# Layer 0's recurrence rates, computed in the projection stage for all tokens and read back from DRAM

## The chip, the cores and the metric

The kernel runs on one core of a Trainium2 chip. Five engines work side by side: PE (TensorE, matmuls), DVE (VectorE), ACT (ScalarE), POOL (GpSimd) and SP (SyncE, which issues the DMAs here). The metric is the device time of one execution in microseconds, median over runs; lower is better. TensorE's clock is granted by a throttle: 1.00 in a row means 2.4 GHz, 0.50 means 1.2 GHz.

## The reference

The program is a block with four mixers and a feed-forward part, then two layers with a mixer and a mixture of experts each. Layer 0's mixer has a recurrence ("rw", of the RWKV-7 kind) beside a latent attention (MLA). The change touches the rates of that recurrence. Cut to it:

```python
def rwkv_prep(p, prm):
    p = centred_shift_mix(p, prm['mu'])
    r, k, v, w1f, w1b, a1f, a1b, g1 = jnp.split(p, RW_SPLITS, axis=-1)
    ...
    for d, (w1, a1) in enumerate(((w1f, a1f), (w1b, a1b))):
        z = (prm['w0'][d] + jnp.tanh(w1) @ prm['w2'][d]).astype(jnp.float32)
        decay = jnp.exp(-jnp.exp(-jax.nn.softplus(-z) - 0.5))
        a = jax.nn.sigmoid((prm['a0'][d] + a1 @ prm['a2'][d]).astype(jnp.float32))
        k_d = kf * (1.0 + (a - 1.0) * prm['k_a'])
        dirs.append((heads(decay), heads(k_d), -kk, kk * heads(a)))
    g = jax.nn.sigmoid(g1) @ prm['g2']
    return heads(r), heads(v), dirs, g
```

`decay` and `a` are the rates: for each of two directions d, a 64 x 512 matrix turns 64 numbers per token into 512. The kernel computes both sigmoids as tanh(0.5 z), 768 tokens (256 of context, 512 latent), 512 channels in four blocks m of 128.

## The kernel before, in words

Layer 0's mixer (`l0_mixer`) has two stages that matter here.

**The projection stage** (`l0_proj`, about 781 to 1066 us of the trace) multiplies the normed tokens with a wide input matrix, 128 output columns at a time. One `project` is 48 matmuls into one PSUM tile of role `p2` (two tiles of two banks each are all that this role has; `p1` has one-bank tiles). `mixed` then blends each token with its neighbours: ACT makes `mc` from PSUM (L989), DVE `ms` (L992) with a POOL copy of the edges (L994), and DVE the result (L995), which is the last reader of the PSUM tile. The first two projections give `tw` (the tanh'd inputs w1 of both directions, then a1): rows 0 to 63 belong to direction 0, rows 64 to 127 to direction 1. They are stored to DRAM as `twT`. The next one is the gate (`sgh`, `sgl`, then six matmul triples with `g2`, copied by ACT at L1020 and stored to `gtok`), then four for k (k0 to k3, with a small fp32 norm matmul on `ind`, L1056), and so on. In front of each projection `fill` lets one or two pieces of the two layers' ada modulation go (L882: four matmuls of 32 output rows and 512 columns per piece, from weights that arrive by DMA). Weights are split into a high and a low part (`wload`: ACT makes `abw_hi` at L208, DVE `abw_lo` at L209), so every product is three matmuls (L186 to L188).

**The recurrence stage** (`l0_rwkv`, about 1066 to 1540 us) walks over six pairs of chunks j, one pair holding 128 tokens of each direction. `rw_prep(j)` loads r, k1, k2 and kk of the chunk (`ld...`, four DMAs of 256 KB for each direction) and makes `ar` and `bk` from them and the rates, mostly on DVE: L1516, a scan at L1519, exponentials on ACT (L1525, L1527), then L1531 to L1538. The step after it is the gram matmul (L1571, which needs `ar` and `bk`). MLA attention steps (s, L186 to L188, softmax, L1269, L1276) are put between by the order string ORD1, which starts `A0 m2 B0 m1 C0 m1 D0 m1 A1`. The rates of chunk pair j are made by `rw_rates(j)`, called once ahead of the loop and then at the end of `rw_prep(j - 1)`: per pair four DMAs of `tw` (32 KB each) out of `twT`, 16 fp32 matmuls with 64 rows of contraction and 128 columns (L1475; each shows as two records) into PSUM tiles `g`, and 16 tanh of 128x128 (L1480) into the tiles `th0`, `th1`. The matrices `w2` and biases `w0` are loaded by `rw_setup` (L1420 to L1427).

The tile scheduler orders the instructions of each engine within a stage; buffers and data decide what waits.

Of the kernel before, what the change touches and what calls it, by code (L numbers as in the profile page):

```python
# [9 lines left out]
F32 = mybir.dt.float32  # L10
# [3 lines left out]
AF = mybir.ActivationFunctionType  # L14
OP = mybir.AluOpType
# [4 lines left out]
P = 128  # L20
# [65 lines left out]
class Net:  # L86
# [828 lines left out]
    def l0_mixer(self, x, xpool, opool, xd, xs):  # L915


        nc, tc = self.nc, self.tc
        d = self.dram
        T = 768  # L920
# [11 lines left out]
        self.twT = d.tile([2, P, T], F32, name="twT")  # L932
# [4 lines left out]
        with ExitStack() as es:  # L937
# [5 lines left out]
            for t in (0, 1, 3, 4, 2, 5):  # L943
# [3 lines left out]
                pv, ts = pt.rearrange("p (i t) -> p i t", i=4), slice(t * P, (t + 1) * P)  # L947
# [3 lines left out]
    def l0_proj(self, x, xpool):  # L951
        nc, I, tc = self.nc, self.I, self.tc
        T = 768
        w = I["ab_w_in_2"][0]
        with ExitStack() as es:
# [19 lines left out]

            def project(wh, wl, j, m=P):

                self.fill(5)
                o = self.p2()
                for k in range(8):  # L980
                    for (a, b) in ((256, 768), (0, 256)):
                        self.mm3(o[:m, 256 + a:256 + b], wh[:, k, j:j + m], wl[:, k, j:j + m],
                                 hi[:, k, a:b], lo[:, k, a:b], k == 0, k == 7)
                return o[:m, 256:1024]
# [13 lines left out]
            wh, wl = self.wload(w, 8, 256, "abw", c0=12 * P)  # L998
            for j in range(2):
                m = wp.tile([P, T], F32, tag="mx", bufs=3, name="mx")  # L1000
                mixed(project(wh, wl, j * P), 12 + j, m)
                if j == 0:
                    nc.scalar.activation(m, m, AF.Tanh)
                nc.sync.dma_start(self.twT[j], m)
# [339 lines left out]
    def l0_rwkv(self, xd, xs, es):  # L1344
        nc = self.nc

        with ExitStack() as e2:
            self.rc = e2.enter_context(self.pool("rwc", 1))
            self.rw = e2.enter_context(self.pool("rww", 2))
            with self.pool("rwp", 2) as self.rp, self.pool("mla", 1, "right") as mp:  # L1350
# [4 lines left out]
                self.rw_rates(0)  # L1355

# [61 lines left out]
    def rw_setup(self):  # L1418
        nc, I, rc = self.nc, self.I, self.rc
        self.w2 = rc.tile([P, 2, 512], F32, name="w2")  # L1420
        self.w0 = rc.tile([P, 2, 2, 4], F32, name="w0")
        for i, (w, o) in enumerate((("rw_w2_2", "rw_w0_2"), ("rw_a2_2", "rw_a0_2"))):
            nc.sync.dma_start(self.w2[:, i], I[w][0].rearrange("d k n -> (d k) n"))
            src = I[o][0]
            nc.sync.dma_start(self.w0[:, i], bass.AP(tensor=src.tensor, offset=src.offset,
                                                     ap=[[1, P], [512, 2], [P, 4]]))
        nc.vector.tensor_scalar(self.w0, self.w0, 0.5, None, op0=OP.mult)  # L1427
# [32 lines left out]
    def rw_rates(self, j):  # L1460

        nc, rp = self.nc, self.rp
        if j == 6:
            return
        self.rth = []
        for d in range(2):
            seg = self.chunks(2 * j)[d] // 2
            ts, hs = slice(seg * P, (seg + 1) * P), slice(64 * d, 64 * d + 64)
            th = []
            for i in range(2):  # L1470
                tw = rp.tile([P, P], F32, tag=f"tw{i}", bufs=1, name=f"tw{i}")
                nc.sync.dma_start(tw[hs], self.twT[i, hs, ts])
                z = self.pt("g")
                for m in range(4):
                    nc.tensor.matmul(z[:, m * P:(m + 1) * P], self.w2[hs, i, m * P:(m + 1) * P], tw[hs],  # L1475
                                     start=True, stop=True)
                t = rp.tile([P, 512], F32, tag=f"th{i}{d}", bufs=1, name=f"th{i}")
                for m in range(4):
                    cs = slice(m * P, (m + 1) * P)
                    nc.scalar.activation(t[:, cs], z[:, cs], AF.Tanh, scale=0.5, bias=self.w0[:, i, d, m:m + 1])  # L1480
                th.append(t)
            self.rth.append(th)
# [19 lines left out]
    def rw_prep(self, j):  # L1502
# [4 lines left out]
        for d in range(2):  # L1507
# [7 lines left out]
            th, ta = self.rth[d]  # L1515
# [26 lines left out]
        self.rw_rates(j + 1)  # L1542
# [876 lines left out]
```

## Time and profile before

| what | value |
|---|---|
| median of 3 runs | 2537.07 us (2532.33 to 2540.72) |
| the profiled execution | 2529.52 us, span 2527.8 us |
| mean granted clock | 0.929 |
| PE busy | 2277.4 us, 90% of the span |
| DVE, ACT, POOL busy | 1545.7, 1109.3, 321.7 us |

The span is the stretch that the trace covers; the execution's own time is 1.7 us longer. All working is done against the profiled execution, which lies 7.6 us under the median of the runs.

### The profile page before, as it was taken

To read this page: it belongs to the slowest core of one execution; us is meant where nothing else is said; L and a number is where in the kernel's file an instruction comes from. 1 tells how busy PE (TensorE), PEld (TensorE's weight loads), DVE (VectorE), ACT (ScalarE), POOL (GpSimd) and SP (SyncE) were. 2 spreads that over 40 slices of the span, in tenths; PEclk is the share of its full clock that TensorE was granted. 3 is DMA by queue.
4 is the path that set the end of the run, shared out by engine and by line. 5 is a ranking of instruction groups with operands and counts; after the bars stand their busy time and mean duration, and the time that the engine had idled before them with its cause. 6 is when DMAs were issued, how large, how long until landed. Compare 5 with 4: busy or idle time off the path is not lost. (4 is left out here: it accounts for less than half of the span.)

```text
span 2527.8 us, 37507 instructions
## 1 busy us (share of the span) xinstructions
PE 2277.4 (90%) x14345; PEld 1808.3 (72%) x14345; DVE 1545.7 (61%) x2915; ACT 1109.3 (44%) x1836; POOL 321.7 (13%) x409
## 2 busy tenths in 40 slices
PE   8959999999988999988999998898994989998994
PEld 6836577888876677766788886697773767687773
DVE  4455654323324455645676648967876987666885
ACT  4435533212223233433445433336774456624773
POOL 0001201000000000011111114200113113301112
PEclk9979989999999999955999999989997999998997
DMA  5345535233325656453545426639996220056995
GB/s 166 100 166 173 190 136 196 88 109 100 101 61 189 224 191 218 125 125 73 113 112 124 102 59 183 236 130 341 342 340 225 97 67 1 1 171 206 375 365 191
DMA packets 367793, 411.55 MB, mean 163 GB/s; under 512 B 117476, under 2 KB 299172, under 8 KB 361468
## 3 DMA queue, kind: packets, MB, share of 16 engines
q1 hardware_dynamic: 356972, 370.83, 46.4%
q0 software_dynamic: 10640, 38.31, 4.1%
q8 instruction: 114, 1.87, 0.3%
q14 instruction: 67, 0.55, 0.1%
HBM read 340.46 MB, written 70.65 MB: 163 GB/s over the span
## 5 line engine op out<-in xcount | busy, mean ns | idle before, releaser
L304 DVE TENSOR_REDUCE mx<-s 128x1 f32<-128x768 f32 (+4 forms) x160 | 121.4, 760 | 85.9 <-PE s L188 65.3
L209 DVE TENSOR_TENSOR eg_l<-eg_w,eg_h 128x2048 fp32r<-128x2048 f32 x66 | 151.0, 2289 | 19.5 <-ACT eg_h L208 19.3
L208 ACT ACTIVATE eg_h<-eg_w 128x2048 fp32r<-128x2048 f32 x66 | 126.5, 1918 | 28.7 <-DMA eg_w<-in_moe_w_up_dram 12.2
L186 PE MATMUL p<-lhh,abw_hi 128*128 128x512 f32 (+1 forms) x336 | 115.3, 343 | 0.8 <-ACT l0n1tmp L241 0.8
L188 PE MATMUL p<-lhh,abw_lo 128*128 128x512 f32 (+1 forms) x336 | 114.5, 341 | 1.6 <-DVE abw_lo L209 1.6
L187 PE MATMUL p<-lhl,abw_hi 128*128 128x512 f32 (+1 forms) x336 | 114.7, 341 | 0.0
L187 PE MATMUL g<-eg_l,xh 128*128 128x512 f32 x264 | 107.1, 406 | 5.5 <-DVE eg_l L209 5.0
L186 PE MATMUL g<-eg_h,xh 128*128 128x512 f32 x264 | 107.6, 408 | 3.8 <-ACT eg_h L208 3.8
L188 PE MATMUL g<-eg_h,xl 128*128 128x512 f32 x264 | 104.4, 395 | 0.0
L209 DVE TENSOR_TENSOR ed_l<-ed_w,ed_h 128x2048 fp32r<-128x2048 f32 x33 | 75.6, 2292 | 44.1 <-ACT ed_h L208 44.1
L882 PE MATMUL adaps<-adaw,silu_c 128*32 128x512 f32 x384 | 75.3, 640 | 29.6 <-DMA adaw<-in_ada_w_dram 29.6
L994 POOL COPY ms<-mc 128x2 f32<-128x2 f32 x30 | 9.1, 304 | 635.0 <-ACT mc L989 620.1
L2025 POOL DMA_INDIRECT xe<-h2d,idx x33 | 45.9, 1392 | 310.0 <-PE x L2039 243.4
L186 PEld LDWEIGHTS p<-lhh,abw_hi 128*128 128x128 f32 (+1 forms) x336 | 61.8, 184 | 23.9 <-issue 8.0
L310 POOL TENSOR_SCALAR ap<-ap,rc 128x768 f32<-128x768 f32 x64 | 58.4, 913 | 153.7 <-DVE rc L307 92.0
L310 POOL TENSOR_SCALAR mlp<-mlp,rc 128x768 f32<-128x768 f32 (+1 forms) x48 | 41.5, 864 | 250.8 <-DVE rc L307 200.4
L186 PE MATMUL p<-h2h,wg_hi 128*128 128x512 f32 x176 | 69.5, 395 | 0.6 <-ACT h2h L234 0.6
L188 PEld LDWEIGHTS p<-lhh,abw_lo 128*128 128x128 f32 (+1 forms) x336 | 62.3, 185 | 10.1 <-DVE abw_lo L209 2.0
L187 PE MATMUL p<-h2l,wg_hi 128*128 128x512 f32 x176 | 69.1, 393 | 0.0
L188 PE MATMUL p<-h2h,wg_lo 128*128 128x512 f32 x176 | 69.0, 392 | 0.0
L186 PE MATMUL p<-wd_hi,ah 128*128 128x512 f32 x176 | 68.5, 389 | 0.2 <-DVE x L836 0.2
L186 PE MATMUL p<-h2h,wu_hi 128*128 128x512 f32 x176 | 68.7, 390 | 0.0
(750 smaller groups left out, 6770.4 us busy)
## 6 DMA issues: line engine op xcount, KB each, us to landing
adaw<-in_ada_w_dram SPq DMA_DIRECT2D x48, 1024.0 KB
eg_w<-in_moe_w_gate_dram SPq DMA_DIRECT2D x66, 512.0 KB
eg_w<-in_moe_w_up_dram SPq DMA_DIRECT2D x66, 512.0 KB
ed_w<-in_moe_w_down_dram SPq DMA_DIRECT2D x33, 1024.0 KB
yslot<-ye SPq DMA_DIRECT2D x33, 512.0 KB
wg_w<-in_w_gate_up_dram SPq DMA_DIRECT2D x11, 1024.0 KB
wu_w<-in_w_gate_up_dram SPq DMA_DIRECT2D x11, 1024.0 KB
wd_w<-in_w_down_dram SPq DMA_DIRECT2D x10, 1024.0 KB
```

Of the source, the lines that this page charges most:

```text
L186: mm(out, lh, rh, start=start, stop=False)
L187: mm(out, lh, rl, start=False, stop=False)
L188: mm(out, ll, rh, start=False, stop=stop)
L208: self.nc.scalar.activation(hi, raw, AF.Copy)
L209: self.nc.vector.tensor_sub(lo, raw, hi.bitcast(F32))
L304: nc.vector.tensor_reduce(mx, s, axis=AX.X, op=OP.max, negate=True)
L310: nc.gpsimd.tensor_scalar(pout, pout, rc, 1.0, op0=OP.mult, op1=OP.mult)
L882: nc.tensor.matmul(self.ada_ps[32 * j:32 * j + 32], self.silu_c[:, k], w[:, j * 512:(j + 1) * 512], start=k == 0, stop=k == 7, tile_positi ...
L994: nc.gpsimd.tensor_copy(s[:, a:b:b - a - 1], c[:, a + 1:b - 1:b - a - 3])
L2025: nc.gpsimd.indirect_dma_start(out=x, out_offset=None, in_=h2, in_offset=bass.IndirectOffsetOnAxis(ap=idx, axis=0))
```

## The change

The two `tw` tiles stay in SBUF, in the projection stage's pool `kp`. `w2` and `w0` are loaded in that stage. A generator makes the rates of all 768 tokens there: eight steps, one for each rate i and channel block m. A step takes both PSUM tiles of role p2 (one for each direction), runs four fp32 matmuls (512 and 256 columns for each direction, in an order written out by hand), two tanh of 128x768 into a tile `th` with two buffers, and stores both (384 KB each) to `thT` in DRAM. `project` pulls two steps ahead of each projection, from the gate on; so the eight steps stand at four boundaries: before the gate, k0, k1 and k2. The recurrence loads `th0` and `th1` of its chunk from `thT` (four DMAs of 256 KB for each pair in the place of four of 32 KB).

```diff
-        self.twT = d.tile([2, P, T], F32, name="twT")
+        self.thT = d.tile([2, 2, 512, T], F32, name="thT")
...
+            rates = iter(())
+
             def project(wh, wl, j, m=P):
 
                 self.fill(5)
+                for _ in range(2):
+                    next(rates, None)
                 o = self.p2()
...
+            tw = [kp.tile([P, T], F32, name=f"tw{j}") for j in range(2)]
             for j in range(2):
-                m = wp.tile([P, T], F32, tag="mx", bufs=3, name="mx")
-                mixed(project(wh, wl, j * P), 12 + j, m)
+                mixed(project(wh, wl, j * P), 12 + j, tw[j])
                 if j == 0:
-                    nc.scalar.activation(m, m, AF.Tanh)
-                nc.sync.dma_start(self.twT[j], m)
+                    nc.scalar.activation(tw[j], tw[j], AF.Tanh)
+            rates = self.rw_rates(tw, kp)
...
-                self.rw_rates(0)
...
+    def rw_rates(self, tw, wp):
...
+        for i in range(2):
+            for m in range(4):
+                ms = slice(m * P, (m + 1) * P)
+                z = [self.p2() for _ in range(2)]
+                with self.tc.manual_schedule(engines={mybir.EngineType.PE}):
+                    for a, b in ((256, 768), (0, 256)):
+                        for d in range(2):
+                            hs = slice(64 * d, 64 * d + 64)
+                            nc.tensor.matmul(z[d][:, 256 + a:256 + b], w2[hs, i, ms], tw[i][hs, a:b], start=True,
+                                             stop=True)
+                for d in range(2):
+                    t = wp.tile([P, 768], F32, tag="th", bufs=2, name="th")
+                    nc.scalar.activation(t, z[d][:, 256:1024], AF.Tanh, scale=0.5, bias=w0[:, i, d, m:m + 1])
+                    nc.sync.dma_start(self.thT[i, d, ms], t)
+                yield
...
-            th, ta = self.rth[d]
+            th, ta = [rp.tile([P, 512], F32, tag=f"th{i}{d}", bufs=1, name=f"th{i}") for i in range(2)]
+            for i, x in enumerate((th, ta)):
+                nc.sync.dma_start(x.rearrange("p (m t) -> p m t", m=4),
+                                  self.thT[i, d, :, ts].rearrange("(m p) t -> p m t", p=P))
...
-        self.rw_rates(j + 1)
```

Where the instructions stand shows first on PE at the end of the second projection (a1, PSUM tile 287). Before, the gate's projection (tile 288) follows at once:

```order
L187 MATMUL p2_287_5853<-lhl_5591,abw_hi_5774 128x256
L188 MATMUL p2_287_5853<-lhh_5590,abw_lo_5775 128x256
L186 MATMUL p2_288_5924<-lhh_5590,abw_hi_5912 128x512
L187 MATMUL p2_288_5924<-lhl_5591,abw_hi_5912 128x512
L188 MATMUL p2_288_5924<-lhh_5590,abw_lo_5913 128x512
L186 MATMUL p2_288_5924<-lhh_5590,abw_hi_5912 128x256
```

Of the change, at the same place of PE (L1473 are the rates, L882 ada pieces, tile 292 the gate's projection):

```order
L188 MATMUL p2_287_5852<-lhh_5590,abw_lo_5775 128x256
L1473 MATMUL p2_288_5929<-tw0_5779,w2_5922 128x512
L882 MATMUL adaps10_5781<-adaw_6087,silu_c_76 32x512 x4
L1473 MATMUL p2_289_5930<-tw0_5779,w2_5922 128x512
L1473 MATMUL p2_288_5929<-tw0_5779,w2_5922 128x256
L1473 MATMUL p2_289_5930<-tw0_5779,w2_5922 128x256
L1473 MATMUL p2_290_5944<-tw0_5779,w2_5922 128x512
L1473 MATMUL p2_291_5945<-tw0_5779,w2_5922 128x512
L1473 MATMUL p2_290_5944<-tw0_5779,w2_5922 128x256
L1473 MATMUL p2_291_5945<-tw0_5779,w2_5922 128x256
L882 MATMUL adaps10_5781<-adaw_6093,silu_c_76 32x512 x4
L186 MATMUL p2_292_5959<-lhh_5590,abw_hi_5910 128x512
```

Two steps of rates now stand between the two projections; tile 289 is the PSUM buffer of tile 287, which `mixed` reads, tiles 290 and 291 are those that the first step's tanh read, and tile 292 is 290's.

The second place is the fourth boundary on PE, between k1 (tile 310) and k2 (tile 317), of the change; before, k2's projection follows k1's there with ada pieces (L882) and norm matmuls (L1056, now L1060) let in among its own:

```order
L1473 MATMUL p2_313_6321<-tw1_5780,w2_5922 128x512
L882 MATMUL adaps11_6622<-adaw_6629,silu_c_76 32x512 x3
L882 MATMUL adaps11_6622<-adaw_6694,silu_c_76 32x512 x4
L1473 MATMUL p2_314_6322<-tw1_5780,w2_5922 128x512
L1473 MATMUL p2_313_6321<-tw1_5780,w2_5922 128x256
L1060 MATMUL p1_311_6303<-mx_6301,ind_6077 32x512
L1060 MATMUL p1_312_6306<-mx_6301,ind_6077 32x256
L1473 MATMUL p2_314_6322<-tw1_5780,w2_5922 128x256
L1473 MATMUL p2_315_6336<-tw1_5780,w2_5922 128x512
L882 MATMUL adaps11_6622<-adaw_6765,silu_c_76 32x512
L1473 MATMUL p2_316_6337<-tw1_5780,w2_5922 128x512
L1473 MATMUL p2_315_6336<-tw1_5780,w2_5922 128x256
```

The same pattern, with the ada pieces and the norm matmuls moved in between the rates' matmuls. On ACT the order here is: the split of the next weights (`abw_hi`, L208), then `mc` of k1, then the tanh of tile 313.

The third place is PE's start of the recurrence stage. Before (L1475 are the rates, s an MLA score, z a state product, g_393 the first gram):

```order
L1475 MATMUL g_384_8427<-tw1_8425,w2_8358 128x128 x4
L1475 MATMUL g_385_8493<-tw0_8491,w2_8358 128x128 x4
L1669 MATMUL z_489_10508<-S0_8381,ar_8452 128x128 x4
L1475 MATMUL g_386_8505<-tw1_8503,w2_8358 128x128 x4
L1269 MATMUL s_389_8547<-ident_69,mlp_8551 128x128 x2
L1475 MATMUL g_387_8517<-tw0_8515,w2_8358 128x128 x4
L186 MATMUL s_390_8565<-mlak_8543,mlaq_8563 128x256
...
L1475 MATMUL g_388_8529<-tw1_8527,w2_8358 128x128 x4
L1669 MATMUL z_490_10509<-S1_8383,ar_8479 128x128 x2
L1571 MATMUL g_393_8634<-ar_8452,bk_8453 128x128 x4
```

Of the change, the same place (L1570 is the gram, L1668 z, L1273 the turned softmax):

```order
L188 MATMUL s_397_8577<-mlak_8571,mlaq_8575 128x256
L1273 MATMUL s_397_8577<-ident_69,mlp_8581 128x128 x2
L1668 MATMUL z_489_10458<-S0_8499,ar_8526 128x128 x4
L1570 MATMUL g_401_8664<-ar_8526,bk_8527 128x128 x4
L186 MATMUL s_398_8595<-mlak_8573,mlaq_8593 128x256
L187 MATMUL s_398_8595<-mlak_8573,mlaq_8593 128x256
L188 MATMUL s_398_8595<-mlak_8573,mlaq_8593 128x256
L1570 MATMUL g_402_8672<-ar_8526,bk_8527 128x128 x4
L1668 MATMUL z_490_10459<-S1_8501,ar_8557 128x128 x4
```

The eight groups of four rate matmuls (two pairs' worth) are gone from ahead of the first gram; MLA's first score stands first, and the gram comes between the scores of the first and the second.

## Rows read from the trace of the kernel before

**Rows 1.** The page: span.

```profile
span 2527.8 us, 37507 instructions
```

**Rows 2.** Windows: start:end, length, then busy us of PE, PEld, DVE, ACT, POOL, PEclk, DMA share, GB/s.

```profile
807.00:893.00 86.00, 83.79 (x454) 58.64 (x452) 39.52 (x64) 29.73 (x41) 4.05 (x10) 1.00 0.67 222
893.00:1066.00 173.00, 173.00 (x1002) 135.42 (x1002) 101.37 (x227) 62.90 (x91) 6.08 (x20) 1.00 0.57 177
...
1081.00:1108.00 27.00, 21.71 (x89) 18.98 (x90) 16.38 (x30) 12.50 (x39) 1.92 (x5) 0.50 0.69 176
1108.00:1138.00 30.00, 29.63 (x164) 24.15 (x164) 13.48 (x30) 12.28 (x33) 4.15 (x6) 0.50 0.28 64
...
1151.00:1200.00 49.00, 39.08 (x220) 31.28 (x220) 24.76 (x61) 15.54 (x35) 5.33 (x8) 0.53 0.30 68
1200.00:1300.00 100.00, 93.73 (x1204) 78.96 (x1204) 75.27 (x189) 48.01 (x118) 16.26 (x25) 1.00 0.50 114
```

**Rows 3.** Timelines of PE, ACT and DVE at the ends of two projections (start, us, ..., wait).

```profile
798.51 0.29 PE L188 MATMUL p<-lhh,abw_lo 128*128 128x256 f32 x1
...
801.59 1.02 DVE L995 SCALAR_TENSOR_TENSOR mx<-p,mu,ms 128x768 f32<-128x768 f32 x1 [0.28 <-POOL ms L994]
807.19 1.91 ACT L208 ACTIVATE abw_hi<-abw_w 128x2048 fp32r<-128x2048 f32 x1 [7.05 <-PE p L187]
...
812.75 1.02 DVE L995 SCALAR_TENSOR_TENSOR mx<-p,mu,ms 128x768 f32<-128x768 f32 x1 [0.28 <-POOL ms L994]
```

**Rows 4.** Timeline of PE after the second of these projections.

```profile
811.48 0.50 PE L188 MATMUL p<-lhh,abw_lo 128*128 128x512 f32 x1 [1.59 <-DVE abw_lo L209]
```

**Rows 5.** Groups by line, 781 to 893 us: the tanh of 128x768.

```profile
L1003 ACT ACTIVATE mx<-mx 128x768 f32<-128x768 f32 x1 | 0.8, 847 | 2.6 <-DVE mx L995 2.6
```

**Rows 6.** Timelines of PE: fp32 matmuls, an ada pair, and paired 64-row fp32 matmuls.

```profile
846.44 1.06 PE L882 MATMUL adaps<-adaw,silu_c 128*32 128x512 f32 x8
...
873.45 5.43 PE L1080 MATMUL p<-nsb,indT 128*128 128x512 f32 x16
...
1320.30 1.15 PE L1638 MATMUL h<-dst,H 64*64 64x64 f32 x32
```

**Rows 7.** Timeline of ACT: the gate's copies wait for a store.

```profile
820.95 1.21 ACT L1020 ACTIVATE st<-p 128x512 f32<-128x512 f32 x2 [1.99 <-DMA gtok<-st]
```

**Rows 8.** Windows at the start of the stage, columns as in the second group.

```profile
772.00:774.00 2.00, 0.00 (x0) 0.00 (x0) 1.49 (x2) 1.97 (x4) 0.00 (x0) 0.94 0.88 351
774.00:776.00 2.00, 1.97 (x10) 1.34 (x14) 2.00 (x6) 1.47 (x3) 0.00 (x0) 0.50 0.44 104
776.00:778.00 2.00, 2.00 (x14) 0.70 (x7) 1.54 (x4) 1.94 (x5) 0.00 (x0) 0.71 1.08 379
```

**Rows 9.** Windows of the rates' matmuls alone (L1475): PE, PEld, PEclk, DMA share, GB/s.

```profile
1081.00:1108.00 27.00, 15.22 (x64) 13.52 (x64) 0.50 0.69 176
...
1138.00:1151.00 13.00, 7.56 (x32) 6.97 (x32) 0.50 0.39 90
...
1200.00:1400.00 200.00, 14.65 (x96) 11.78 (x96) 1.00 0.51 116
```

**Rows 10.** Timelines of PE, DVE and SP at the recurrence's start.

```profile
1081.73 3.78 PE L1475 MATMUL g<-tw,w 64*128 64x128 f32 x16 [8.30 <-DMA tw<-twT]
...
1107.80 3.09 PE L1571 MATMUL g<-ar,bk 64*128 64x128 f32 x16 [0.39 <-ACT th L1480]
...
1085.02 0.43 DVE L1516 TENSOR_SCALAR th<-th 128x512 f32<-128x512 f32 x1 [2.87 <-ACT th L1480]
...
1092.90 0.69 DVE L1537 TENSOR_TENSOR bk<-ldk,th 128x512 f32<-128x512 f32 x1 [3.56 <-ACT th L1527]
...
1102.53 0.69 DVE L1538 TENSOR_TENSOR ldr<-ldr,ldk 128x512 f32<-128x512 f32 x1
...
1082.59 0.51 SPq L1513 DMA_DIRECT2D ldkk<-kkT  x1
```

**Rows 11.** A window inside the stretch 1151 to 1200, columns as in the second group.

```profile
1180.00:1182.00 2.00, 1.86 (x10) 1.40 (x10) 0.11 (x1) 0.28 (x1) 0.44 (x2) 1.00 0.38 63
```

More of the change, by code (lines that the diff above doesn't have):

```diff
@@ L1419, in rw_setup @@
         nc, I, rc = self.nc, self.I, self.rc
[L1420 to L1427, printed above, removed]
         rwm = rc.tile([P, 320], F32, name="rwm")
@@ L1458, in chunks @@
         return k, (3 - k if k < 4 else 15 - k)
[L1460 to L1482, printed above, removed]
+    def rw_rates(self, tw, wp):
+        nc, I = self.nc, self.I
+        w2 = wp.tile([P, 2, 512], F32, name="w2")
+        w0 = wp.tile([P, 2, 2, 4], F32, name="w0")
+        for i, (w, o) in enumerate((("rw_w2_2", "rw_w0_2"), ("rw_a2_2", "rw_a0_2"))):
+            nc.sync.dma_start(w2[:, i], I[w][0].rearrange("d k n -> (d k) n"))
+            src = I[o][0]
+            nc.sync.dma_start(w0[:, i], bass.AP(tensor=src.tensor, offset=src.offset, ap=[[1, P], [512, 2], [P, 4]]))
+        nc.vector.tensor_scalar(w0, w0, 0.5, None, op0=OP.mult)
+        for i in range(2):
[13 more added lines that the diff above has]
+                yield
```

## The prediction, made blind

> **What bounds the kernel now.** I read the page first, then windows stage by stage, then the timelines of single engines where the change puts or takes something. The reader should see three things. In the projection stage PE is the bound: it is busy for the whole of 893 to 1066 us, at a granted clock of 1.00 [rows 2]; whatever is added to PE there, or makes PE wait there, lengthens the run one for one. In the middle of the recurrence PE is the bound too, 93.73 us of 100 at 1.00 [rows 2]. Between, from 1081 to about 1200 us, PE runs at 0.50, the lower of its two levels, although from 1108 to 1138 it is busy for 29.63 of 30 us [rows 2]. What is taken from PE in that stretch is worth twice its price at 1.00. The change so moves matmuls from a place where PE is the bound at either clock to another where it is the bound at full clock.
>
> **What the recurrence gives back.** The rates' matmuls take 15.22 us of PE in 1081 to 1108, 7.56 in 1138 to 1151, and 14.65 in 1200 to 1400 [rows 9], 37.4 in all.
>
> The start (1081 to 1108) is a chain rather than a sum. PE first waits 8.30 us for `tw`; the first gram stands at 1107.80, right behind the last rate group [rows 10]. With the change the gram needs `th`, `ar` and `bk` alone. `th0` and `th1` are issued behind kk, whose load went out at 1082.59 [rows 10]; three loads ahead of it (`w2`, `w0`) are gone and one MLA load comes in front. Some 2 MB at about the 176 GB/s of this stretch [rows 2] is 10 to 12 us behind the first issue at about 1078 for all of it, less for the first direction; I take `th` as landed at about 1086 to 1087, against 1085.02 for the first use of the tanh'd rate before [rows 10]. From there to the first `bk` product took 7.9 us, of which 3.56 were a wait for an exponential that stood behind the tanhs on ACT [rows 10]; those tanhs are gone. So direction 0 is ready at about 1093, and the gram 14 us earlier. But a score of MLA and a state product, about 3 us at this clock, now come between or behind the grams instead of ahead of them. That leaves 11. Bounds: 5, if direction 1, whose DVE work ended at 1103.2 [rows 10] and whose k1, k2 and kk are loaded last, sets the pace; 15, the rate matmuls themselves.
>
> The second piece (7.56) lies at half clock in a stretch where PE hardly waits; I take 6.5. The third (14.65) is at full clock with PE at 94%; I take 13, the rest going into waits that grow. Bounds for the two together: 15 and 22. ACT loses 96 small tanhs there, off the path. The `th` loads (24 of 256 KB, 6.3 MB, in the place of 24 small ones) run over 300 us in which the DMA share is 0.5 [rows 2, 9], so I cost them at nothing after the start; if that cover is gone, the `th` tiles, which have one buffer each, would hold up DVE's preparation, which runs a pair ahead of the gram. Sum: **-30.5**, between -20 and -37.
>
> **What the projection stage pays.** The matmuls by themselves: eight serial fp32 matmuls, four of 512 and four of 256 columns, took 5.43 us [rows 6], so 1.36 for a pair of 512 and 256 (0.90 and 0.45). There are 16 pairs: 21.7 us. But a step takes both PSUM tiles of p2, so PE must also wait for those who read them. `mixed` frees the tile 3.8 us after the projection's last matmul (798.80 to 802.61) and, when the split of the next weights gets ahead of it on ACT (1.91), and then on DVE, 6.6 us after it (807.2 to 813.77) [rows 3]. A tanh of 128x768 takes 0.85 [rows 5]. A pair of ada pieces takes 1.06 [rows 6], and they run in the gaps.
>
> - *Before the gate.* First direction 0.0 to 0.9, ada piece, then a wait until 3.8 for the tile that `mixed` reads; second direction's 512 to 4.7, both 256s to 5.6 (direction 0 done at 5.2); tanh 5.2 to 6.05 and to 6.9. Second step 6.05 to 8.75, its first tanh waiting to about 9 for the store of the first step out of the two `th` buffers: the gate's copies, likewise with two buffers, waited 1.99 us for a store of 256 KB [rows 7]. The gate's projection starts at about 10.7; the ada pieces in this, nearly 3 us, are done before as well. Net 7.8.
> - *Before k0.* The same two steps, but the six gate products, with their copies on ACT and a weight split of 1.91, now stand between the halves of the first step. I come to 16.9 from end to start, of which 4.2 are gate products, 2 ada pieces, and 1.6 a stall that PE had there before anyway [rows 4]. Net 9.1.
> - *Before k1.* As the first, with norm matmuls in a gap. Net 7.
> - *Before k2.* The weight split stands ahead of `mc` on ACT, so the second direction waits until 6.6, and PE, with 2.6 us of work to put in, stands for 4. The step ends at about 9.8, the next at 12.7. Net 9.5.
>
> Sum: **+33.4**. From below, if the waits were all filled by other work, 21.7; from above, with each wait 2 us longer for a late store, 42. The next things late are the projections' results, but everything behind them in the stage waits for PE anyway. The 16 stores (6.3 MB) go through SP's queue beside ada's loads, at a DMA share of 0.57 [rows 2]; I cost them at nothing apart from the buffer wait.
>
> One row speaks for cheaper matmuls: 32 records, 16 fp32 matmuls of 64 columns that alternate between the two halves of the array's rows, took 1.15 us [rows 6], 0.072 each, where 0.90 x 64/512 would be 0.11. So halves overlap in part. In my walk that saves only about 0.5 at each boundary, since the tanhs and `mixed` set the pace: 31 instead of 33, which I leave inside the range.
>
> The Trainium skill ("TensorE: Matmul & The Clock Gate", Part 3: Packing small matmuls) goes further: matmuls in different row groups run at the same time. By that the two directions would cost as one, the matmuls 10.9 us and not 21.7, and the walk again about 31; the row shows about a third saved and not half.
>
> **The sum.** -30.5 + 33.4 = +2.9, so 2532.4 for the profiled execution (2529.5, 1.7 above its span [rows 1]) and **2540** for the median of the runs shown, which lies 7.6 higher. 0.3%, 7.6 us, is about what a measurement of this kernel can tell from no change.
>
> **The rivals.**
> - *The half-clock stretch ends earlier (faster).* In 1151 to 1200 PE has 39.08 busy us at 0.53 [rows 2]; the clock was back for a moment at 1180 [rows 11], after a dense run of MLA's products, and for good at about 1200. Without the rates' matmuls and their waits, the dense run before that one, at about 1153, might already bring it back. At full clock these 39 us are about 20: another -19, so 2521. For it: the change takes the waiting and thin work out from ahead of this place. Against it: 1108 to 1138 was as good as full and stayed at 0.50 [rows 2], and the change takes nothing from there. It decides from about 10 us of earlier rise on.
> - *The clock falls at the boundaries (slower).* At 772 PE stood still, and from 774 on the clock was 0.50 for two us and 0.71 for two more [rows 8]. PE's gaps at the boundaries are 3 to 4 us. A fall that costs 1.6 us each is +6; one after the fourth that lasts for a projection of 8.5 us, +8 more. I take +10: 2550. It decides from +5 on, where 2540 leaves the 0.3%. The Trainium skill has the rule behind it ("TensorE: Matmul & The Clock Gate", Part 1: the clock gate): the gate halves the clock by how busy PE has lately been. Rows 8 agree; how large a gap is enough, no row here shows.
> - *The rates' loads come late (slower).* 256 KB in the place of 32 KB where the DMA share is already 0.69 [rows 2]: `th` lands at 1097 rather than 1087 and the start gives nothing. +11: 2551.
> - *Row halves overlap and the boundaries fill better.* -6: 2534.
>
> **How the numbers follow.** My sum 0.45 (its own range 2531 to 2550; faster 0.03, same 0.30, slower 0.12), the earlier clock 0.20 (faster 0.19), the falling clock 0.17 (slower 0.16), late loads 0.10 (slower 0.09), better filling 0.08 (same 0.06, faster 0.02); what is left of each lies within 0.3%. Faster 0.24, same 0.39, slower 0.37. Range 2520 to 2560: it takes in all five, and leaves out the far ends of the costs.
>
> **What would show it.** In the new profile: four gaps in the projection stage with PE waiting for DVE and ACT, and this stage longer by 33; the first gram of the recurrence some 11 us nearer to the stage's start; 20 us less PE in what follows; ACT and DVE no longer waiting for rates. It is wrong if the stage grows by under 25 or over 42, if the clock in the stage is under 1.00, or if the half-clock stretch after the start changes its length by more than 10.

## The result, and the profile after

The changed kernel takes 2568.0 us (median of 4 runs, 2561.56 to 2577.89) against 2538.9 of the kernel before on the same chip: ratio 1.0127, 95% interval 1.0099 to 1.0156. It is slower by 29 us, where 2540, a change of 3 us, was forecast, and it lies outside the range. Its profiled execution took 2562.12 us, 32.6 more than that of before.

```profile
span 2560.4 us, 37211 instructions
```

The two stages are best read as one window each: from the first to the last input-projection matmul, and from there to the last product of MLA's output matrix, which ends layer 0's mixer. Windows of the kernel before (start:end, length, busy us of PE, PEld, DVE, ACT, POOL, PEclk, DMA share, GB/s):

```profile
781.57:1065.84 284.27, 282.06 (x1595) 216.12 (x1596) 147.98 (x302) 98.05 (x140) 10.88 (x34) 1.00 0.57 181
1065.84:1588.34 522.50, 468.15 (x4933) 391.87 (x4931) 331.83 (x788) 225.04 (x496) 96.42 (x119) 0.87 0.48 116
```

The same two windows of the changed kernel, and then pieces of the first:

```profile
782.99:1111.45 328.46, 313.98 (x1659) 229.76 (x1660) 148.36 (x305) 111.57 (x156) 12.22 (x36) 0.95 0.54 175
1111.45:1620.95 509.50, 428.52 (x4743) 355.09 (x4742) 335.44 (x796) 199.69 (x402) 94.77 (x120) 0.89 0.51 130
...
800.00:812.00 12.00, 9.94 (x38) 3.54 (x40) 2.85 (x4) 4.96 (x6) 0.38 (x2) 0.72 0.62 240
812.00:824.00 12.00, 11.62 (x66) 7.90 (x58) 0.63 (x1) 2.58 (x2) 0.00 (x0) 1.00 0.71 240
824.00:836.00 12.00, 7.64 (x16) 4.63 (x17) 5.24 (x6) 3.61 (x6) 1.71 (x2) 0.57 0.63 220
836.00:870.00 34.00, 32.02 (x153) 19.77 (x152) 6.99 (x10) 12.41 (x16) 0.38 (x2) 1.00 0.71 248
870.00:885.00 15.00, 10.67 (x37) 2.82 (x35) 6.13 (x7) 6.20 (x7) 1.71 (x2) 0.77 0.64 237
```

The projection stage is 44.2 us longer (33.4 were forecast), the recurrence stage 13.0 shorter (30.5 were forecast). The remaining 1.4 of the 32.6 lie ahead of the first window; what follows the second sums to nothing.

**Projection.** PE is busy for 31.9 us more and idle for 12.3 more. The boundaries show in its timeline (line 1473 is the rates' matmul, each shown as two records; the wait for DVE's line 999 is the wait for `mixed`):

```profile
804.16 2.28 PE L1473 MATMUL p<-tw,w 64*128 64x512 f32 x6 [1.91 <-DVE tw L999]
...
828.15 2.04 PE L1473 MATMUL p<-tw,w 64*128 64x512 f32 x2 [4.29 <-DVE mx L999]
...
838.99 2.02 PE L1473 MATMUL p<-tw,w 64*128 64x512 f32 x8
...
877.26 2.04 PE L1473 MATMUL p<-tw,w 64*128 64x512 f32 x4 [3.75 <-DVE kt L999]
```

These are three of the four waits for `mixed` that the walk had, and the clock fell at each of the three: 0.72, 0.57 and 0.77 in the pieces above, at the boundaries before the gate, k0 and k2; before k1 no wait is longer than 0.80, and the clock stayed at 1.00. At 828.15 a 512 matmul takes 2.04, at 838.99 a whole step of four takes 2.02. The rates' matmuls alone (PE, PEld, PEclk, DMA share, GB/s), and then the rest of the stage, behind the last boundary:

```profile
782.99:1111.45 328.46, 24.59 (x64) 8.90 (x64) 0.95 0.54 175
885.00:1111.45 226.45, 225.08 (x1266) 176.25 (x1266) 121.66 (x267) 77.83 (x114) 7.17 (x24) 0.98 0.51 162
```

So the rates' matmuls cost 24.59 in this stage, and the other work in it 289.4 (313.98 less 24.59) instead of 282.1. The 0.98 behind the last boundary is a fourth fall, to 0.50 from 934.50 to 941.33, where no rates stand. PE at this place (the norm's matmuls of one column, line 1141 of before and 1145 of the change), of before and of the changed kernel:

```profile
889.78 1.06 PE L882 MATMUL adaps<-adaw,silu_c 128*32 128x512 f32 x6
890.81 1.50 PE L1141 MATMUL p<-ones,sq 128*128 128x1 f32 x12
...
934.51 2.72 PE L1145 MATMUL p<-ones,sq 128*128 128x1 f32 x12 [0.96 <-ACT sq L1140]
```

Before, an ada piece fills the wait for ACT here; in the changed kernel the ada pieces have run at the boundaries, PE waits 0.96 us, and the clock is at the lower level.

**Recurrence.** Its start, to be held against [rows 10], in the timelines of PE, DVE and SP:

```profile
1127.31 0.58 PE L186 MATMUL s<-mlak,mlaq 96*128 96x256 f32 x1 [8.55 <-DMA mlak<-mk]
...
1136.14 2.08 PE L1668 MATMUL z<-S,ar 128*128 128x128 f32 x8 [5.25 <-DVE ar L1532]
1138.55 2.07 PE L1570 MATMUL g<-ar,bk 64*128 64x128 f32 x8 [0.33 <-DVE bk L1534]
...
1131.83 0.43 DVE L1516 TENSOR_SCALAR th<-th 128x512 f32<-128x512 f32 x1 [2.25 <-DMA th<-thT]
...
1125.30 2.55 SPq L1514 DMA_DIRECT2D th<-thT  x2
```

The first gram stands 27.1 us behind the last projection matmul, before 42.0: 14.9 gained, where 11 were forecast, although the rate arrives later (20.4 us into the stage, before 19.2). DVE waits for a load of `th` only this once in the whole stage, 2.25 us, so late loads are not what holds it. But then nothing more comes: the first MLA score gains 9.4 against the end of the projections (15.9 us behind it, before 25.3), the last of 80 scores 7.4 (428.6 and 436.0), so from the first score to the last it takes 412.7 for 410.8. Between these two PE's busy time falls from 383 to 361 us and its idle time rises from 27.5 to 51.7. PE's waits in the whole stage, longest first (line 1269 of before is 1273 of the change: the transposes of the softmax), of before:

```profile
PE g L1475 <- DMA tw<-twT: 12.5, 3, 8.3
PE s L1269 <- POOL mlp L310: 9.8, 13, 3.3
```

and of the changed kernel:

```profile
PE s L1273 <- POOL mlp L310: 26.1, 20, 4.3
PE s L186 <- DMA mlak<-mk: 8.6, 1, 8.6
PE g L187 <- DVE mol L209: 6.7, 2, 5.1
```

What the rates' matmuls filled is now mostly a wait for MLA's softmax: of the 26.7 us by which PE's idle time grows in the stage, 16.3 are in its line.

### The profile page after: what moved, and what is told of

It is laid out like the page before. It is cut to its first block, busy times and chain, and to the rows that moved or that the text cites. A ratio compares the mean times of both kernels' runs of the same rounds, so it can differ in the third digit from the quotient of the medians.

```text
span 2560.4 us, 37211 instructions
## 1 busy us (share of the span) xinstructions
PE 2270.9 (89%) x14217; PEld 1787.6 (70%) x14217; DVE 1547.6 (60%) x2915; ACT 1096.5 (43%) x1756; POOL 319.5 (12%) x409
## 5 line engine op out<-in xcount | busy, mean ns | idle before, releaser
L208 ACT ACTIVATE eg_h<-eg_w 128x2048 fp32r<-128x2048 f32 x66 | 126.6, 1920 | 29.4 <-DMA eg_w<-in_moe_w_up_dram 13.4
L882 PE MATMUL adaps<-adaw,silu_c 128*32 128x512 f32 x384 | 78.2, 641 | 35.3 <-DMA adaw<-in_ada_w_dram 34.5
L188 PE MATMUL p<-wd_hi,al 128*128 128x512 f32 x176 | 68.5, 389 | 0.0
```

Source lines behind the costliest of these rows:

```text
L188: mm(out, ll, rh, start=False, stop=stop)
L208: self.nc.scalar.activation(hi, raw, AF.Copy)
L882: nc.tensor.matmul(self.ada_ps[32 * j:32 * j + 32], self.silu_c[:, k], w[:, j * 512:(j + 1) * 512], start=k == 0, stop=k == 7, tile_positi ...
```

## The experiments

Two numbers stand for a run where its time alone doesn't tell: the lengths of the two windows above, 284.3 and 522.5 for before, 328.5 and 509.5 for the changed kernel. The recurrence stage of one and the same program differs by its clock, so I also multiply its length by its mean granted clock. That product is only a rough length at 2.4 GHz, since waits don't shrink with the clock: 455 for before (522.5 x 0.87), 453 for the change (509.5 x 0.89).

### The gain alone, and the cost alone

The first leaves out the rates' matmuls and tanhs in the projection stage and stores stand-in numbers:

```diff
-                z = [self.p2() for _ in range(2)]
...
                 for d in range(2):
-                    t = wp.tile([P, 768], F32, tag="th", bufs=2, name="th")
-                    nc.scalar.activation(t, z[d][:, 256:1024], AF.Tanh, scale=0.5, bias=w0[:, i, d, m:m + 1])
-                    nc.sync.dma_start(self.thT[i, d, ms], t)
+                    nc.sync.dma_start(self.thT[i, d, ms], tw[i])
```

> The changed kernel without its fp32 rate matmuls and their tanhs in the projection stage: the same 16 stores of 384 KB go to DRAM, but straight from the tw tiles, so the recurrence reads stand-in numbers in the place of rates. What is left against the kernel before is the recurrence's gain, and the DMAs. Theory A (the projection stage pays all of its 46 us for matmuls, waits and a falling clock, and the recurrence gives back only about 9 at its start and 4 behind it, because PE there waits for MLA's softmax as soon as the rates are out of its way): projection stage as long as before, about 285 us from 781 us to its last projection matmul, time 11 to 15 under before, ratio about 0.995. Rival B (the recurrence would give back the forecast 30, and only what the projection stage leaves behind, a lower clock and late loads, eats it): 25 to 32 under before, ratio about 0.988 to 0.990.

The second is the kernel before, with the changed kernel's steps (as a function of another name) in its projection stage, and `twT` still written and read.

> The rates made in both places: in the projection stage and stored as in the changed kernel, and in the recurrence as before, which alone uses them. Theory A: the projection stage pays its 46 us and nothing comes back, ratio about 1.018. By the forecast's price of 33.4 for the stage: 1.013. If it came out under 1.010, the stage's price in the changed kernel would have come from something else than the rates.

Windows of the first:

```profile
790.88:1076.50 285.62, 282.56 (x1595) 215.86 (x1596) 148.17 (x302) 98.12 (x140) 11.55 (x34) 1.00 0.62 200
1076.50:1591.20 514.70, 431.81 (x4742) 358.03 (x4742) 337.65 (x796) 200.02 (x402) 94.74 (x120) 0.88 0.51 129
...
1900.00:2000.00 100.00, 42.30 (x126) 30.07 (x126) 46.40 (x56) 33.51 (x44) 18.73 (x18) 0.65 0.48 178
```

Its time, 2581.1 us, ratio 1.0156 (1.0116 to 1.0197), can't be used: behind the second window it takes 987.1 us where before takes 939.5, and in the part shown last PE is busy for only 42.30 of 100 us (59.91 in the kernel before). The stand-ins probably change what the router of the experts sees; no run shows that this is the reason. The stages can be used. The 16 stores of 6.3 MB cost next to nothing (285.6 for 284.3), and the recurrence without rates gives back 7.8 in length, weighted 453. That falls short of theory A's 11 to 15, and is nothing like B's 25 to 32.

The cost alone, 2589.5 us, ratio 1.0162 (1.0092 to 1.0231):

```profile
786.43:1115.49 329.06, 314.28 (x1659) 229.94 (x1660) 148.65 (x306) 111.74 (x156) 12.17 (x36) 0.95 0.55 178
```

The stage pays 44.8, as in the changed kernel; the recurrence stage, 529.0 at 0.87, is that of before, 6 longer. So the cost is real and was measured twice, and what the changed kernel gives back against it is small.

### Waits and clock at the boundaries

Rates in one-bank PSUM tiles that no `mixed` reads:

```diff
-                z = [self.p2() for _ in range(2)]
...
+                    t = wp.tile([P, 768], F32, tag="th", bufs=2, name="th")
+                    for a, b in ((0, 512), (512, 768)):
+                        z = self.p1()
+                        nc.tensor.matmul(z[:, :b - a], w2[hs, i, ms], tw[i][hs, a:b], start=True, stop=True)
+                        nc.scalar.activation(t[:, a:b], z[:, :b - a], AF.Tanh, scale=0.5, bias=w0[:, i, d, m:m + 1])
```

> The changed kernel with the rates in one-bank PSUM tiles of role p1 (512 and 256 columns apart, 32 tanhs in the place of 16), so that no rate matmul waits for the tile that mixed still reads. Theory A: PE's gaps of 2 to 4 us at the boundaries go (12.8 us of idle time in the stage), and with them the falls of the clock in this stage (17 us by the busy time of rates and other work): the stage pays about 18 to 25, time 20 to 28 under the changed kernel, ratio to before about 1.002 to 1.005. Rival C (the fp32 matmuls and their tanhs are the price, wherever they stand): the stage still pays 38 or more, ratio 1.010 to 1.013.

2561.9 us, ratio 1.0091 (1.0062 to 1.0120). Its two windows:

```profile
782.57:1094.30 311.73, 305.61 (x1659) 225.43 (x1660) 148.92 (x306) 114.29 (x172) 10.62 (x36) 0.99 0.58 185
1094.30:1616.10 521.80, 440.37 (x4742) 365.40 (x4742) 334.28 (x795) 199.78 (x402) 94.35 (x120) 0.87 0.51 127
```

and the rates' matmuls alone in the first (PE, PEld, PEclk, DMA share, GB/s):

```profile
782.57:1094.30 311.73, 19.50 (x64) 8.38 (x64) 0.99 0.58 185
```

Waits and falls of the clock go together: idle time 14.5 to 6.1, clock 0.95 to 0.99, rates 24.59 to 19.50, the stage 328.5 to 311.7. So 16.7 of the 44.2 were the place of the rates in p2, and C falls by the stage. The stage still pays 27.5, a little over A's 18 to 25, and the time missed A's ratio, since the recurrence stage, the same program as in the changed kernel, took 521.8 here at a clock of 0.87.

The attempt to keep the waits and lift only the clock, with matmuls of no use in the gap:

```diff
+                warm = 18
...
+                            if m % 2 == 0 and a and d:
+                                for k in range(warm):
+                                    nc.tensor.matmul(wz, hi[:, k % 8, :P], hi[:, k % 8, 256:768], start=True, stop=True)
```

> The changed kernel with 18 idle bf16-rate matmuls of 512 columns (about 4.2 us, into a PSUM tile that nobody reads) in each of the four boundaries, between the first direction's matmul and the second's, which waits for mixed. PE's gap is then filled with work of no use. Theory F (about a third of the stage's 45.6 us is the lower clock that follows the gaps: 15.5 us by the granted clock of the stage): the clock stays at 1.00 there, and the stage gets 6 to 14 shorter although it does 17 us more PE work; ratio to before 1.008 to 1.011. Rival G (the waits and the rates' own work are the price, the clock adds little): the stage is as long as in the changed kernel or 2 to 6 longer.

```profile
780.42:1127.71 347.29, 325.34 (x1731) 240.19 (x1732) 148.68 (x305) 112.56 (x156) 12.21 (x36) 0.97 0.52 166
```

2599.4 us, ratio 1.0244 (1.0219 to 1.0269). Theory F missed: PE is busy for 11.4 more, its clock rose from 0.95 to 0.97 only, and its idle time grew by 7.5. Rival G missed as well: the stage is 18.8 longer than in the changed kernel, not 2 to 6. The idle matmuls made new waits: PE waits 10.5 us in two places for ACT at the norm matmuls that now stand ahead of them, and 6.4 for ada's weights. Only at the boundary before the gate did they fill the gap as meant; there the clock stayed at 1.00, and the second step of four (line 1478 here) took half of what it took in the changed kernel:

```profile
805.38 2.02 PE L1478 MATMUL p<-tw,w 64*128 64x512 f32 x8
...
806.60 3.76 PE L1473 MATMUL p<-tw,w 64*128 64x512 f32 x8 [0.15 <-ACT th L1477]
```

So at this one boundary, with the same rates, filling the wait kept the clock up. What the clock alone costs over the stage, this run can't tell, since its waits changed too.

### What holds the recurrence

Two buffers for MLA's softmax tile (`tag="p", bufs=2`):

> The changed kernel with two buffers for MLA's softmax tile (mlp) in the recurrence stage instead of one. Theory A (the recurrence is held by MLA's chain of score, maximum, exponential, POOL's scaling, transposes and products, whose tile is single, once the rates are out): the next score's exponential no longer waits for the transposes of the one before, the stage gets 10 to 20 us shorter, ratio to before about 1.005 to 1.009. Rival D (PE's own work or DVE's preparation sets the pace): within 4 us of the changed kernel, 1.011 to 1.014.

2570.4 us, ratio 1.0121 (1.0077 to 1.0166); recurrence stage 521.9 at 0.86. No gain, as rival D had it by the time (2568.0 for the changed kernel). The score, the transposes and the products of one head go through one PSUM tile `s`, which is single too, so the next head can't start earlier; that this is the reason was not tried by itself.

MLA's scaling on DVE instead of POOL, in both kernels (`nc.vector.tensor_scalar` for `nc.gpsimd.tensor_scalar` in the softmax):

> The changed kernel with MLA's scaling of the softmax (128x768, 0.91 us on POOL, 48 of them) done by DVE instead. Theory A2 (the recurrence stage is as long as MLA's 48 serial heads: score, maximum, exponential, scaling, transposes, copy, products, all through one PSUM tile s, so PE work that is taken away only turns into waits in this chain): a DVE scaling of about 0.56 saves 0.35 and a handover of about 0.2 at each head, so 15 to 27 us from the first score to the last (412.7 in the changed kernel), the time 15 to 27 under the changed kernel, ratio to before about 1.003 to 1.008. Rival E (PE's order, or DVE, already busy 272 of 429 us and now with 27 more, sets the pace): no shorter, or longer, ratio 1.012 or more.

> The same move of the scaling to DVE in the kernel before, rates in the recurrence. Theory A2 (MLA's chain set the stage before the change too, which is why the rates' matmuls there cost next to nothing): 10 to 25 us shorter, ratio 0.990 to 0.996. Rival E (before the change PE was the bound of this stage, as the prediction had it): within 4 us of before, or longer by what DVE gets.

In the changed kernel 2569.7 us, ratio 1.0130 (1.0107 to 1.0153); in the kernel before 2558.1, 1.0087 (1.0057 to 1.0117). Their recurrence stages:

```profile
1106.80:1617.00 510.20, 434.26 (x4742) 360.71 (x4742) 349.78 (x845) 199.43 (x402) 50.73 (x71) 0.87 0.52 130
```

```profile
1067.75:1603.05 535.30, 474.89 (x4935) 397.04 (x4934) 351.23 (x845) 225.44 (x498) 51.53 (x72) 0.85 0.47 114
```

No forecast of A2 came in: neither got shorter than its own kernel's stage, the second even 12.8 longer. Weighted they are 444 and 455, so with the rates out there is a trace of a gain, with the rates in none. The first is best held against the run with p1 tiles, whose recurrence is the changed kernel's, at the same clock of 0.87: 510.2 against 521.8.

A second scaling by 1.0 on POOL, in the kernel before:

> The kernel before with MLA's scaling on POOL followed by a second one by 1.0, which changes no number and gives POOL 48 more instructions of about 0.9 (40 us in all) and PE, DVE and ACT nothing. Theory A2 (MLA's chain sets the stage in the kernel before): the stage gets 30 to 43 us longer, ratio 1.012 to 1.017. Rival E (PE was the bound, MLA's chain has slack): under 12 us longer, ratio under 1.005.

2568.0 us, ratio 1.0144 (1.0102 to 1.0186). From the first score to the last 449.4 instead of 410.8; the stage 549.1 at 0.86, weighted 472. The ratio and the 38.6 from score to score are what A2 forecast, the stage, 26.6 longer, a little less than its 30. From first to last gram the time is 340.2 for 337.0, so it is MLA's chain that got longer and ended later: it has no slack.

MLA left out of both kernels (a constant is stored in the place of its results):

> The changed kernel with MLA's scores, softmax and products left out of the recurrence (a constant is stored in the place of each result, so later stages see other numbers, and only the recurrence stage is compared). Beside the next run it shows what the rates cost there when MLA's chain is gone. Theory A2: without MLA this stage is shorter than that of the next run by 15 to 30 us, since the rates' work is then no longer covered. Rival E: the two differ by under 10, as they do with MLA.

> The kernel before with MLA left out in the same way. Theory A2: this stage is 15 to 30 us longer than that of the changed kernel without MLA, in full-clock time. Rival E: under 10.

Recurrence stages without and with the rates:

```profile
1116.30:1566.80 450.50, 336.08 (x3829) 286.82 (x3827) 288.89 (x700) 124.74 (x234) 56.49 (x95) 0.79 0.49 122
```

```profile
1066.20:1533.30 467.10, 373.59 (x4020) 322.16 (x4019) 289.48 (x699) 151.16 (x329) 59.43 (x95) 0.77 0.44 107
```

16.6 apart, as A2 had it, but 13.0 of these are the 26.2 and 39.2 us that pass before the first gram, and from the first gram to the last they take 297.5 and 297.6. Their first and last grams, without the rates and then with them:

```profile
1142.49 3.10 PE L1540 MATMUL g<-ar,bk 64*128 64x128 f32 x16 [0.34 <-DVE bk L1504]
...
1440.00 1.22 PE L1540 MATMUL g<-ar,bk 64*128 64x128 f32 x4
...
1105.37 3.09 PE L1541 MATMUL g<-ar,bk 64*128 64x128 f32 x16
...
1402.95 1.22 PE L1541 MATMUL g<-ar,bk 64*128 64x128 f32 x4
```

So between the grams the rates cost nothing even without MLA, and A2 falls as the only cover. What covers them there is probably the recurrence's own hand-overs between PE, ACT and DVE; no run singles them out.

The rates' matmuls of the pairs 2 to 5 issued twice, in the kernel before:

```diff
-                for m in range(4):
+                for m in [0, 1, 2, 3] * (2 if j >= 2 else 1):
                     nc.tensor.matmul(z[:, m * P:(m + 1) * P], self.w2[hs, i, m * P:(m + 1) * P], tw[hs],
...
```

> The kernel before with the rates' fp32 matmuls of the pairs 2 to 5 issued twice into the same PSUM tile, so PE gets the 22 us of these matmuls once more and nothing else changes. Theory H (in the recurrence PE's work fills waits that hand-overs between the engines set anyway, so rate matmuls cost little there): first to last gram under 8 us longer than before's 337.0 after the granted clock is taken into account, ratio to before under 1.004. Rival E (PE's work is the bound of this stage, as the prediction had it): 16 to 22 longer, ratio 1.006 to 1.009.

2560.3 us, ratio 1.0092 (1.0058 to 1.0125); the stage:

```profile
1069.51:1623.11 553.60, 497.06 (x5060) 415.97 (x5059) 342.31 (x791) 224.43 (x497) 104.18 (x125) 0.86 0.45 111
```

Theory H falls: from first to last gram 357.8 instead of 337.0, at nearly the same clock (0.86 and 0.87). Rival E's 16 to 22 came in: PE's matmuls of the rates take 55.9 us for 37.4, so 18.5 more PE work costs 20.8 there and 31.1 over the stage. So PE has no slack either, and yet less PE work doesn't shorten the stage. The next two leave MLA's scaling out (later stages see other numbers):

> The changed kernel with POOL's scaling of MLA's softmax left out (48 instructions of about 0.9 us in MLA's chain; later stages see other numbers, so only the recurrence stage is compared). Theory J (two limits close together: PE's work and the hand-over chain of MLA; the change shortened the first alone): first to last score 15 to 30 shorter than the changed kernel's 412.7, in full-clock time (365.7 there) too. Rival K (a third limit, the recurrence's own chain or DVE, holds the stage): under 8 shorter.

> The kernel before with the same scaling left out. Theory J: PE's work, with the rates in it, still holds the stage, so it is under 8 shorter than the 410.8 of before (357.8 in full-clock time). If it gets shorter by 15 or more, MLA's chain alone was the bound before the change, and then the 21 us for doubled rates must have another cause.

Recurrence stages without and with the rates:

```profile
1115.93:1612.73 496.80, 429.88 (x4742) 356.77 (x4742) 327.52 (x798) 198.91 (x401) 51.41 (x71) 0.88 0.53 133
```

```profile
1067.67:1587.27 519.60, 473.02 (x4932) 395.56 (x4931) 329.89 (x788) 223.57 (x496) 52.16 (x71) 0.87 0.48 117
```

By the measure on record, first to last score, both got shorter (374.8 and 388.2), the changed kernel by 37.9, the kernel before by 22.6, which J had excluded. So by its own forecast J missed. That measure ends with MLA's scores: MLA ends earlier, and what stands behind it takes longer: 106.8 us from the last score to the stage's end in the kernel before, where it took 86.5, and 105.9 for 80.9 in the changed kernel. Over the whole stage the changed kernel gains 12.7 (weighted 453 to 437), the kernel before 2.9 (455 to 452). That is J's pattern, but by a measure chosen after the runs and in one profile each, where the recurrence of the kernel before took 522.5 in one run and 529.0 in another (the cost alone).

### Only what stands ahead of the first gram

The kernel before, with the rates of the first pair, or the first two, made in the projection stage in p1 tiles, one or two groups ahead of each of four projections, and loaded as `th`:

```diff
+                    z = self.p1()
+                    t = wp.tile([P, 512], F32, tag="th", bufs=2, name="th")
+                    for m in range(4):
+                        nc.tensor.matmul(z[:, m * P:(m + 1) * P], w2[hs, i, m * P:(m + 1) * P], tw[i][hs, ts],
+                                         start=True, stop=True)
...
+                    nc.sync.dma_start(self.thT[j, i, d], t)
```

> The kernel before with the rates of the first chunk pair alone made in the projection stage (four groups of four fp32 matmuls of 128 columns, one group ahead of each of four projections, in PSUM tiles of role p1 that wait for nobody) and loaded by the recurrence; all other pairs as before. Theory A2 (taking the rates out pays at the recurrence's start alone, where PE waits for them in a chain; further on they lie beside MLA's chain): the projection stage pays 3 to 5, the start gives 4 to 9, the time 1 to 6 under before, ratio 0.997 to 1.000. Rival: the projection stage pays again with a lower clock, or the clock in the recurrence falls further, ratio over 1.003.

> The same with the first two chunk pairs, all that stood ahead of the first gram: eight groups, two ahead of each of the four projections. Theory A2: the projection stage pays 7 to 10, the start gives the changed kernel's 9 to 10, ratio 0.998 to 1.002. Rival as in the run with one pair: ratio over 1.004.

One pair: 2541.7 us, ratio 1.0014 (0.9997 to 1.0030); the projection stage pays 5.2 (289.5), the first gram comes 4.2 earlier in its stage (37.8 for 42.0), and the time doesn't change. Two pairs: 2557.6, ratio 1.0079 (1.0051 to 1.0107); 10.7 paid, 13.6 gained at the first gram, and the stage then took 533.1 at 0.86, 10.6 longer than before: the rival's ratio over 1.004, not A2's. No version that leaves nothing out beats the kernel before.

## Why the prediction was wrong

On the profiled execution the forecast was +2.9 and the result +32.6. Of the difference 17.5 are the recurrence's (13.0 given back for 30.5), 10.8 the projection stage's (44.2 paid for 33.4), and 1.4 lie ahead of it. Three of the signs of being wrong came: the projection stage grew by more than 42, its clock was under 1.00, and the stretch at half clock behind the start changed by more than 10.

**What failed most: that the recurrence behind its start gives back 19.5.** These are the 6.5 and 13 of the sum. The prediction read PE's 93.73 of 100 busy us [rows 2] as a bound, so that each us taken from it comes back. Apart from the start none did: PE's idle time took its place, with MLA (24 us more idle between first and last score) and without it (297.5 and 297.6). Why the row misleads is argued more than shown: the doubled rates and the second scaling fit a stage in which PE's order and the chains of hand-overs lie so close together that lengthening either costs, and shortening one leaves the other. The last pair of runs fits this over the whole stage, on single profiles, though not by the measure put on record for it; the DVE runs fit only where two profiles have the same clock. It is the best-supported reading, and not settled.

**The start** had its mechanism right and its size too small: 14.9 at the first gram for 11. The lateness that a rival feared was there (`th` used 20.4 us into the stage for 19.2), and the shorter DVE chain, without the 3.56 wait [rows 10], outweighed it. But of this only 13.0 is left at the stage's end, in a profile with a clock of 0.89; in two others of the same recurrence program, at 0.87 (521.8) and 0.83 (534.0), next to nothing or less is left.

**The projection's 33.4** had the waits right in sum, 12.3 us of idle time, and three of the four places: before k1 the walk had a wait that didn't come. The term that was mis-sized is the clock, carried as a rival of +10 and a chance of 0.17: the rates' matmuls cost 24.6 and at full clock 19.5, other work 7.3 more, together 12.4. So the 44.2 are 19.5 of matmuls, 12.3 of waits and 12.4 of clock, where the forecast had 21.7 of matmuls, 11.7 of waits and nothing else. The trace gives the same by another way: in the four stretches at 0.50 (804.80 to 811.63, 825.28 to 835.52, 876.48 to 883.30 and 934.50 to 941.33) PE is busy for 26.1 us, half of which is 13. Of this the fall at 934.50, which no boundary of the walk has, is 3.4. So the falling-clock rival deserved more than its chance: [rows 8] had shown what a gap does, and the walk itself had set gaps of 3 to 4 us.

The Trainium skill ("TensorE: Matmul & The Clock Gate", Part 1: The HAM clock gate) has the gate act on how busy PE has lately been. These runs agree in direction: at three boundaries with gaps of 1.91 to 4.29 us the clock fell, at the one without it did not, and with p1 tiles it stayed at 0.99.

**The price of the matmuls** lay between the two readings: a step of 512 and 256 columns for both halves took 2.02 at full clock, where 2.71 is serial. It moved the sum by little, as foreseen. By the Trainium skill (the same page, Part 3: Packing small matmuls), which has matmuls in different row groups run at the same time, an estimate is 1.36; the row shows about half of that saving.

**Stores, loads and ACT** cost next to nothing, as said: 285.6 for 284.3 in the stage with the stores alone, though in the changed kernel one tanh waited 2.5 us for a store, and in the recurrence DVE waited for `th` once.

**The earlier clock**, the rival on the fast side, came in part. The first 200 us of the recurrence, of before and of the changed kernel:

```profile
1065.84:1265.84 200.00, 166.35 (x1325) 137.43 (x1325) 114.32 (x260) 80.58 (x200) 28.62 (x49) 0.68 0.46 108
...
1111.45:1311.45 200.00, 150.24 (x1421) 123.09 (x1419) 120.70 (x284) 69.17 (x147) 31.11 (x53) 0.74 0.54 134
```

0.74 for 0.68 is, by estimate, 24 us less at half clock (0.06 x 200 / 0.5); the rival had the clock back some 47 us earlier. In the run with p1 tiles it was 0.70, and that recurrence gave back 0.7. So the 13.0 of the changed kernel's profile goes with its clock, and at the clock of before there is next to nothing, as far as single profiles tell.

## What to carry to other kernels

An engine that is busy for 94% of a stage is not yet its bound: look at which hand-overs of the other engines it still waits for, and test it by taking work away, since adding work shows a cost in both cases. Moving work out of such a stage into one where the engine is busy without a gap buys it at full price, and where its buffers make the engine wait, with a lower clock on top. Where a chain really waits for the moved work (here the first gram), move that piece alone, and still expect little.

## What the runs showed of the hardware that was not expected

One and the same recurrence program, without the rates, took 509.5, 514.7, 521.8 and 534.0 us in four profiles, with mean clocks of 0.89, 0.88, 0.87 and 0.83 (the changed kernel, the gain alone on stand-in numbers, p1 tiles, idle matmuls). Runs of one kernel between 2561 and 2578 us, with mean clocks of 0.928 to 0.918, fit this. So a gain of 13 us in a stage of 500 can't be read from two profiles without the clock beside it.
